# Where the sums of squares of the SwiGLU norm are made, when the first gate-and-up weights load, and which matmuls stand ahead of the last transposes

## The chip, the cores and the metric

The kernel runs on one core of a Trainium2 chip. The metric is device time in microseconds (us) of one execution; lower is better. Five engines work from queues of their own: TensorE (PE; its weight loads are PEld), VectorE (DVE), ScalarE (ACT), GpSimd (POOL) and SyncE (SP), which issues most transfers. Each runs its instructions in order and waits for the others by semaphores.

## The reference, cut to what matters

Two layers on 512 tokens of width 1024, in float32. Layer 0 mixes tokens with a dilated window attention, layer 1 with a gated linear attention (GLA); both end with a SwiGLU block of hidden width 2816:

```python
def rms_norm(x, gain):
    xf = x.astype(jnp.float32)
    y = xf * lax.rsqrt(jnp.mean(xf * xf, axis=-1, keepdims=True) + RMS_EPS)
    return (y * gain.astype(jnp.float32)).astype(x.dtype)

def swiglu(h, w_gate_up, w_down):
    g, u = jnp.split(h @ w_gate_up, 2, axis=-1)
    return (jax.nn.silu(g) * u) @ w_down

# in reference(), for each layer i
    h = h + mix.astype(h.dtype)
    h = h + swiglu(rms_norm(h, ffn_norm[i]), ffn_w_gate_up[i], ffn_w_down[i]).astype(h.dtype)
```

## The kernel before

**Products.** Each large product is float32 made of two halves: a hi half that ScalarE writes (a copy, L92) and a lo half that VectorE writes (source minus hi, L93). `split` makes both, and each block costs three matmuls: hi by hi, hi by lo, lo by hi (`mm3`, L104 to L106; `product`, L298 to L300).

**Layout.** The residual h lies transposed, as eight tiles of 128 features by 512 tokens. In `swiglu`, `gate_up` makes the hidden activations, `down` brings them back.

**The start of the block.** As each tile of h is finished (the attention's last adds at L767, the GLA's at L423), `enter_blocks` writes its gained operands (ScalarE L180, VectorE L181, tag xs), and `add_square` squares it on ScalarE (L151) and adds it on GpSimd to one tile, acc (L152). The norm's factor is applied to the products later, so the products don't wait for it by their data. `token_norm` sums acc over features with small matmuls (L205) into pt and makes R, the factor by token, in small steps on ScalarE and VectorE (L110 to L115, L208, L210). `block_sums` makes the sums of operands that the seven products need (ScalarE L192; VectorE L194 to L197, tag g; halves in sh and sl).

**Seven products.** `gate_up` runs six chunks of columns (five of 512, one of 256). In each, with tokens in halves and features in halves, seven products take the place of eight: A11 by first, A12 by second, then S1 by fifth, S2 by sixth, S4 by third, S3 by seventh, A22 by fourth, 24 matmuls each. `forms` makes the seven weights: SyncE loads blocks (wA, wf, wB), GpSimd's DMAs add a block into one that is there (L236), VectorE adds two (L267), and each is split. A load, add or split of `forms` gets a priority offset of AHEAD = 100 over what is written around it; a scheduler orders each engine's instructions from priorities and dependences. SiLU (L359, L381), the products with R (L371, L383) and the transposes of the activations (`turn`, L324, with a copy to an act at L330) follow; transposes of a chunk are made while the next chunk is multiplied. The token norm is called after the second product's matmuls of chunk 0; the scheduler puts its matmuls where acc allows. Three buffers each hold wh and wl, two wB.

**Down.** After chunk 5's last SiLU, `turn` transposes that chunk's two columns of blocks, and `down` splits all 22 activations (tag ah) and runs 66 matmuls for each of eight output tiles m, adding h, which is read back from DRAM (L408). In layer 0 each result enters the next mixer's norm, `enter_norm`, with `add_square` again.

## Time and profile before

| what | value |
|---|---|
| time of three runs | 1593.56, 1594.47, 1595.35 us; median 1594.47 |
| the profiled execution | 1593.73 us, its span 1592.0 us |
| mean granted TensorE clock | 0.991 |
| GpSimd's adds of squares (L152) | 21, 30.7 us together |
| ScalarE's squares (L151) | 21, 13.1 us together |
| transposes of activations (L324) | 176, 30.2 us together (16.4 + 13.8) |

Durations below are those of one profiled execution. A row of the timeline gives start, duration, engine, line, operation, what is written from what, and, in brackets, how long the engine was idle before it and what it waited for. A matmul's shown duration is its passage through the array; the distance between starts is what one costs. The granted clock is a share of full speed.

### The profile page before, as it was taken

To read this page: it belongs to the slowest core of one execution; us is meant where nothing else is said; L and a number is where in the kernel's file an instruction comes from. 1 tells how busy PE (TensorE), PEld (TensorE's weight loads), DVE (VectorE), ACT (ScalarE), POOL (GpSimd) and SP (SyncE) were. 2 spreads that over 40 slices of the span, in tenths; PEclk is the share of its full clock that TensorE was granted. 3 is DMA by queue.
4 is the path that set the end of the run, shared out by engine and by line. 5 is a ranking of instruction groups with operands and counts; after the bars stand their busy time and mean duration, and the time that the engine had idled before them with its cause. 6 is when DMAs were issued, how large, how long until landed. Compare 5 with 4: busy or idle time off the path is not lost.

```text
span 1592.0 us, 21064 instructions
## 1 busy us (share of the span) xinstructions
PE 1552.2 (97%) x8078; PEld 1258.5 (79%) x8078; DVE 947.0 (59%) x1693; ACT 779.0 (49%) x1319; POOL 134.3 (8%) x201
## 2 busy tenths in 40 slices
...
GB/s 277 139 73 88 69 79 87 60 121 97 80 67 48 70 44 178 126 159 159 159 160 113 125 100 85 95 67 66 67 69 215 136 154 158 155 149 123 113 120 65
DMA packets 58964, 179.74 MB, mean 113 GB/s; under 512 B 9936, under 2 KB 10512, under 8 KB 58864
## 3 DMA queue, kind: packets, MB, share of 16 engines
...
## 4 chain that ended last, share of the span: by engine, by line
PE 73%; issue 12%; DVE 7%; ACT 3%; DMA 2%; POOL 2%; SPq 0%; POOLq 0%; DVEq 0%; ACTq 0%
PE ppp L496 8%; PE ppp L494 8%; PE ppp L495 8%; PE ppp L105 7%; PE ppp L104 7%; PE ppp L106 7%; PE po L603 4%; PE ppp L298 3%; PE ppp L299 3%; PE ppp L300 3%; DMA wB<-in_gate_up_dram 2%; PE ps L671 2%; DVE wl L93 2%; PE pt L541 2%; PE ps L621 1%
## 5 line engine op out<-in xcount | busy, mean ns | idle before, releaser
L93 DVE TENSOR_TENSOR wl<-wf,wh 128x1024 fp32r<-128x1024 f32 (+1 forms) x180 | 214.7, 1193 | 212.2 <-ACT wh L92 211.2
L92 ACT ACTIVATE wh<-wf 128x1024 fp32r<-128x1024 f32 (+1 forms) x180 | 185.5, 1031 | 305.9 <-PE ppp L105 181.2
L494 PE MATMUL ppp<-wh,xs 128*128 128x512 f32 (+1 forms) x672 | 263.0, 393 | 5.6 <-ACT wh L92 5.6
L496 PE MATMUL ppp<-wh,xs 128*128 128x512 f32 (+1 forms) x672 | 262.8, 391 | 0.0
L495 PE MATMUL ppp<-wl,xs 128*128 128x512 f32 (+1 forms) x672 | 262.6, 391 | 0.0
L494 PEld LDWEIGHTS ppp<-wh,xs 128*128 128x128 f32 x672 | 128.0, 191 | 30.4 <-ACT wh L92 5.6
L496 PEld LDWEIGHTS ppp<-wh,xs 128*128 128x128 f32 x672 | 127.9, 190 | 23.4 <-issue 0.2
L495 PEld LDWEIGHTS ppp<-wl,xs 128*128 128x128 f32 x672 | 128.2, 191 | 22.2 <-DVE wl L93 1.2
L104 PE MATMUL ppp<-ah,wh 128*128 128x512 f32 x352 | 138.1, 393 | 2.2 <-ACT ah L92 2.2
L105 PE MATMUL ppp<-ah,wh 128*128 128x512 f32 x352 | 138.5, 394 | 0.5 <-DVE ah L93 0.5
L106 PE MATMUL ppp<-ah,wl 128*128 128x512 f32 x352 | 138.0, 392 | 0.0
L93 DVE TENSOR_TENSOR wl<-wA,wh 128x1024 fp32r<-128x1024 f32 x88 | 107.5, 1221 | 50.1 <-ACT wh L92 50.0
L92 ACT ACTIVATE wh<-wA 128x1024 fp32r<-128x1024 f32 x88 | 92.6, 1056 | 53.1 <-PE ppp L300 39.0
L299 PE MATMUL ppp<-wl,xs 128*128 128x512 f32 (+1 forms) x288 | 108.2, 376 | 1.2 <-DVE wl L93 1.2
L298 PE MATMUL ppp<-wh,xs 128*128 128x512 f32 (+1 forms) x288 | 108.5, 383 | 0.0
L300 PE MATMUL ppp<-wh,xs 128*128 128x512 f32 (+1 forms) x288 | 107.7, 375 | 0.0
L93 DVE TENSOR_TENSOR wl<-wB,wh 128x1024 fp32r<-128x1024 f32 x44 | 53.9, 1225 | 89.5 <-ACT wh L92 89.5
L105 PE MATMUL ppp<-xs,wh 128*128 128x512 f32 x224 | 91.1, 407 | 1.0 <-DVE xs L93 1.0
L104 PE MATMUL ppp<-xs,wh 128*128 128x512 f32 x224 | 91.1, 407 | 0.0
L106 PE MATMUL ppp<-xs,wl 128*128 128x512 f32 x224 | 90.2, 403 | 0.0
L104 PEld LDWEIGHTS ppp<-ah,wh 128*128 128x128 f32 x352 | 66.6, 189 | 16.5 <-ACT ah L92 2.7
L105 PEld LDWEIGHTS ppp<-ah,wh 128*128 128x128 f32 x352 | 66.9, 190 | 15.8 <-DVE ah L93 2.0
...
## 6 DMA issues: line engine op xcount, KB each, us to landing
...
```

Source lines behind the costliest of these rows:

```text
L92: nc.scalar.activation(hi, src, AF.Copy)
L93: nc.vector.tensor_sub(lo, src, hi.bitcast(F32))
L104: mm(out, lhsT=wh, rhs=xh, start=start, stop=False)
L105: mm(out, lhsT=wh, rhs=xl, start=False, stop=False)
L106: mm(out, lhsT=wl, rhs=xh, start=False, stop=stop)
L298: mm(a, lhsT=xh[:, tok], rhs=wh[:, f], start=start and k == 0, stop=False, skip_group_check=True)
L299: mm(a, lhsT=xh[:, tok], rhs=wl[:, f], start=False, stop=False, skip_group_check=True)
L300: mm(a, lhsT=xl[:, tok], rhs=wh[:, f], start=False, stop=k == last, skip_group_check=True)
L494: mm(a, lhsT=xh, rhs=wh[:, f], start=k == 0, stop=False)
L495: mm(a, lhsT=xh, rhs=wl[:, f], start=False, stop=False)
L496: mm(a, lhsT=xl, rhs=wh[:, f], start=False, stop=k == KT - 1)
L603: self.nc.tensor.matmul(o, lhsT=pts[b][c], rhs=vals(i0 + b, c), start=c == 0, stop=c == 1)
```

## The change

Three edits. (1) `enter_blocks` makes no squares; `gate_up` makes them in chunk 0 after the second product, in two buffers by turns (sq and R), and the add to acc is VectorE's, here and in layer 0's `down`. (2) Chunk 0's first weights get a priority offset of 300 instead of 100. (3) The first two activations are split in chunk 1's part of the program order, written at the end of chunk 4, into free xs buffers, and the six down matmuls on them for m = 0 are issued ahead of the last transposes; `down_part` holds the loop that `down` had.

```diff
--- before.py
+++ after.py
@@ -52,7 +52,7 @@
             "qv": 2, "qr": 2, "qtmp": 2, "st": 2, "t2": 2, "stn": 2, "st0": 2, "mw": 2, "mL": 5}
     FFN = {"a": NH - KT}
     GATE_UP = {"sh": 4, "sl": 4, "wA": 4, "wB": 2, "g": 7, "Rc": 8}
-    DOWN = {"ah": 2 * NH}
+    DOWN = {"ah": 2 * NH - 4}
     GLA = {"qk": 8, "r": 8, "v": 8, "wg": 1, "z": 1, "rs": 2, "A": 2, "qs": 6, "kT": 6, "e": 4, "y": 1, "c": 1, "wa": 3,
            "state": 6, "later": 1, "reset": 1, "Rc": 1, "mid": 2, "full": 4}
     PBUFS = {"pp": 4, "s": 2, "t": 1, "o": 1}
@@ -141,15 +141,15 @@
         self.x[m] = self.gained(src, col)
         self.add_square(m, src)
 
-    def add_square(self, m, src):
+    def add_square(self, m, src, tag="sq"):
         nc = self.nc
         if m == 0:
             self.acc = self.t("acc")
             nc.scalar.activation(self.acc, src, AF.Square)
         else:
-            sq = self.t("sq")
+            sq = self.t(tag)
             nc.scalar.activation(sq, src, AF.Square)
-            nc.gpsimd.tensor_add(self.acc, self.acc, sq)
+            nc.vector.tensor_add(self.acc, self.acc, sq)
 
     def column_sums(self, ps, src):
         hi, lo = self.split(src, (P, S), "e", "e")
@@ -180,7 +180,6 @@
         nc.scalar.activation(xh, part, AF.Copy, scale=col)
         nc.vector.scalar_tensor_tensor(xl, part, col, xh.bitcast(F32), op0=ALU.mult, op1=ALU.subtract)
         self.x[m] = (xh, xl)
-        self.add_square(m, src)
 
     def block_sums(self, m):
         nc = self.nc
@@ -219,7 +218,7 @@
             with self.phase(f"down{layer}", self.DOWN):
                 self.down(layer, acts, col_next)
 
-    def forms(self, dram):
+    def forms(self, dram, ahead=0):
         nc = self.nc
         n = dram.shape[1]
         raw = {}
@@ -280,8 +279,9 @@
             return ready("wA")
 
         for step in (first, second, fifth, sixth, third, seventh, fourth):
-            with self.tc.high_priority(offset=AHEAD):
+            with self.tc.high_priority(offset=AHEAD + ahead):
                 w = step()
+            ahead = 0
             yield w
 
     def product(self, acc, x, w, width, start):
@@ -303,7 +303,7 @@
         nc = self.nc
         self.col0 = 16 + 8 * layer
         ACT, DVE = nc.scalar.activation, nc.vector
-        weights = [self.forms(self.ins["gate_up"][layer, j]) for j in range(5)]
+        weights = [self.forms(self.ins["gate_up"][layer, j], 0 if j else 2 * AHEAD) for j in range(5)]
         weights.append(self.forms(self.ins["gate_up_last"][layer]))
         first = next(weights[0])
         self.minus = self.t("Rc", (P, 8))
@@ -350,6 +350,8 @@
             self.product(b2, A12, next(w), width, True)
             turn(1)
             if j == 0:
+                for m in range(KT):
+                    self.add_square(m, self.h[m], ("sq", "R")[m % 2])
                 R = self.token_norm()
                 for m in range(KT):
                     nc.gpsimd.dma_start(self.kept[m], self.h[m])
@@ -382,28 +384,41 @@
                 u = h2[:, i, 0:width]
                 DVE.scalar_tensor_tensor(u, u, R[:, 6 + i:7 + i], e, op0=ALU.mult, op1=ALU.mult)
             done = (h1, h2)
+            if j == 4:
+                with self.tc.high_priority(offset=AHEAD):
+                    early = [self.split(a, (P, S), "xs", "xs") for a in acts[0:2]]
+        self.started = self.down_part(self.p("pp"), layer, 0, 0, 2, early)
         for c in range(2):
             turn(c)
         with self.tc.issue_after(silu.ins):
             nc.scalar.preload_act_table_set("natural_log_exp_and_others")
 
+    def down_part(self, ps, layer, m, k, end, pairs):
+        for k0, kn in ((0, 8), (8, 8), (16, 6)):
+            if k0 <= k < min(end, k0 + kn):
+                if k == k0:
+                    self.down_w = self.weight(self.ins["down"][layer, m, :, k0 * P:(k0 + kn) * P], kn * P)
+                wh, wl = self.down_w
+                while k < min(end, k0 + kn):
+                    c = slice((k - k0) * P, (k - k0 + 1) * P)
+                    self.mm3(ps, wh[:, c], wl[:, c], *pairs[k], k == 0, k == NH - 1)
+                    k += 1
+        return ps, pairs
+
     def down(self, layer, acts, col_next):
         nc = self.nc
-        pairs = []
-        for k, a in enumerate(acts):
+        ps, pairs = self.started
+        for k in range(2, NH):
             if k < 8:
                 with self.tc.high_priority(offset=AHEAD):
-                    pairs.append(self.split(a, (P, S), "ah", "ah"))
+                    pairs.append(self.split(acts[k], (P, S), "ah", "ah"))
             else:
-                pairs.append(self.split(a, (P, S), "ah", "ah"))
+                pairs.append(self.split(acts[k], (P, S), "ah", "ah"))
         self.x = [None] * KT
         for m in range(KT):
-            ps = self.p("pp")
-            for k0, kn in ((0, 8), (8, 8), (16, 6)):
-                wh, wl = self.weight(self.ins["down"][layer, m, :, k0 * P:(k0 + kn) * P], kn * P)
-                for k in range(k0, k0 + kn):
-                    c = slice((k - k0) * P, (k - k0 + 1) * P)
-                    self.mm3(ps, wh[:, c], wl[:, c], *pairs[k], k == 0, k == NH - 1)
+            if m > 0:
+                ps = self.p("pp")
+            self.down_part(ps, layer, m, 2 if m == 0 else 0, NH, pairs)
             h = self.t("h")
             nc.sync.dma_start(h, self.kept[m])
             self.h[m] = h
```

Lines after some 150 shift by one to three, and `down` by more. The following rows are each engine's order in the program, without times: line, operation, what is written from what.

TensorE at the start of `gate_up` in layer 0, before: the attention's last matmul, the token norm (pt from ones and acc), the first product.

```order
L106 MATMUL ppp_1123_5917<-qk_1051_5577,wl_1110_5869 128x512
L205 MATMUL pt_1161_6065<-ones_4_73,acc_1098_5822 128x1 x4
L298 MATMUL ppp_1150_5998<-wh_1129_5943,xs_1097_5819 128x512
L298 MATMUL ppp_1151_5999<-wh_1129_5943,xs_1097_5819 128x512
L299 MATMUL ppp_1150_5998<-wl_1130_5944,xs_1097_5819 128x512
L300 MATMUL ppp_1150_5998<-wh_1129_5943,xs_1097_5819 128x512
```

After the change the first product follows the attention directly:

```order
L106 MATMUL ppp_1116_5897<-qk_1051_5577,wl_1106_5858 128x512
L298 MATMUL ppp_1142_5975<-wh_1121_5920,xs_1097_5819 128x512
L298 MATMUL ppp_1143_5976<-wh_1121_5920,xs_1097_5819 128x512
L299 MATMUL ppp_1142_5975<-wl_1122_5921,xs_1097_5819 128x512
L300 MATMUL ppp_1142_5975<-wh_1121_5920,xs_1097_5819 128x512
```

and the token norm stands inside product S4 (acc pair ps, operands sh):

```order
L300 MATMUL ps_1165_6093<-wh_1179_6175,sl_1133_5949 128x512
L298 MATMUL ps_1166_6094<-wh_1179_6175,sh_1132_5948 128x512
L204 MATMUL pt_1161_6065<-ones_4_73,acc_1153_6042 128x1 x4
L299 MATMUL ps_1166_6094<-wl_1180_6176,sh_1132_5948 128x512
L300 MATMUL ps_1166_6094<-wh_1179_6175,sl_1133_5949 128x512
L298 MATMUL ps_1165_6093<-wh_1181_6179,sh_1136_5959 128x512
```

The token norm moved back by 106 rows, from ahead of the first product into the fifth that is issued.

VectorE in the same chunk, at products S1 to S4, before (wl and sl are lo halves of weights and operand sums, Rc the norm's small tiles):

```order
L93 TENSOR_TENSOR wl_1175_6139<-wA_1127_5939,wh_1174_6138 128x1024
L93 TENSOR_TENSOR sl_1149_5994<-g_1147_5988,sh_1148_5993 128x1024
L93 TENSOR_TENSOR wl_1177_6143<-wA_1128_5941,wh_1176_6142 128x1024
L208 TENSOR_SCALAR Rc_1162_6070<-pt_1161_6065 128x4
L358 TENSOR_TENSOR g_1152_6024<-ppp_1153_6027,g_1152_6024 128x512
L358 TENSOR_TENSOR g_1152_6024<-ppp_1154_6028,g_1152_6024 128x512
L93 TENSOR_TENSOR wl_1180_6176<-wB_1167_6097,wh_1179_6175 128x1024
L93 TENSOR_TENSOR wl_1182_6180<-wB_1168_6099,wh_1181_6179 128x1024
```

and after:

```order
L93 TENSOR_TENSOR sl_1141_5971<-g_1139_5965,sh_1140_5970 128x1024
L93 TENSOR_TENSOR wl_1175_6139<-wA_1119_5916,wh_1174_6138 128x1024
L93 TENSOR_TENSOR wl_1177_6143<-wA_1120_5918,wh_1176_6142 128x1024
L152 TENSOR_TENSOR acc_1153_6042<-acc_1153_6042,R_1156_6050 128x512
L93 TENSOR_TENSOR wl_1180_6176<-wB_1167_6097,wh_1179_6175 128x1024
L152 TENSOR_TENSOR acc_1153_6042<-acc_1153_6042,sq_1157_6053 128x512
L360 TENSOR_TENSOR g_1144_6001<-ppp_1145_6004,g_1144_6001 128x512
L152 TENSOR_TENSOR acc_1153_6042<-acc_1153_6042,R_1158_6056 128x512
L93 TENSOR_TENSOR wl_1182_6180<-wB_1168_6099,wh_1181_6179 128x1024
L152 TENSOR_TENSOR acc_1153_6042<-acc_1153_6042,sq_1159_6059 128x512
L360 TENSOR_TENSOR g_1144_6001<-ppp_1146_6005,g_1144_6001 128x512
L152 TENSOR_TENSOR acc_1153_6042<-acc_1153_6042,R_1160_6062 128x512
```

Five adds to acc stand between the low halves of the weights, and sl of the fourth operand sum stands one low half sooner.

ScalarE in chunk 0 of layer 1, before (wh from wB is the hi half of S4's weights first; ACT_TABLE_LOAD changes the table of functions):

```order
L110 ACT_TABLE_LOAD
L110 ACTIVATE Rc_2034_10575<-Rc_2033_10574 128x4
L92 ACTIVATE wh_2047_10646<-wA_1999_10445 128x1024
L111 ACT_TABLE_LOAD
L111 ACTIVATE Rc_2034_10575<-Rc_2034_10575 128x4
L342 ACTIVATE g_2044_10637<-ps_2036_10597 128x512
L92 ACTIVATE wh_2050_10679<-wB_2038_10601 128x1024
L342 ACTIVATE g_2044_10637<-ps_2037_10598 128x512
L359 ACT_TABLE_LOAD
L359 ACTIVATE g_2023_10528<-g_2023_10528,Rc_2034_10575 128x512
L92 ACTIVATE wh_2052_10683<-wB_2039_10603 128x1024
```

and after:

```order
L92 ACTIVATE wh_2045_10642<-wA_1990_10420 128x1024
L92 ACTIVATE wh_2047_10646<-wA_1991_10422 128x1024
L342 ACTIVATE g_2044_10637<-ps_2036_10597 128x512
L92 ACTIVATE wh_2050_10679<-wB_2038_10601 128x1024
L342 ACTIVATE g_2044_10637<-ps_2037_10598 128x512
L92 ACTIVATE wh_2052_10683<-wB_2039_10603 128x1024
L110 ACT_TABLE_LOAD
L110 ACTIVATE Rc_2034_10575<-Rc_2033_10574 128x4
L342 ACTIVATE g_2049_10674<-ppp_2013_10479 128x512
L111 ACT_TABLE_LOAD
```

Both hi halves of wB stand ahead of the table loads now.

TensorE at the end of `gate_up` and the start of `down` in layer 0, before:

```order
L300 MATMUL ppp_1406_7508<-wh_1440_7745,xs_1125_5926 128x256
L324 MATMUL pt_1443_7778<-ident_2_65,g_1434_7676 128x128
L324 MATMUL po_1445_7785<-ident_2_65,g_1434_7676 128x128 x2
L324 MATMUL pt_1443_7778<-ident_2_65,g_1439_7740 128x128
L324 MATMUL po_1445_7785<-ident_2_65,g_1439_7740 128x128
L324 MATMUL pt_1443_7778<-ident_2_65,g_1439_7740 128x128
L324 MATMUL po_1445_7785<-ident_2_65,g_1439_7740 128x128
L104 MATMUL ppp_1491_7885<-ah_1447_7797,wh_1493_7888 128x512
L105 MATMUL ppp_1491_7885<-ah_1448_7798,wh_1493_7888 128x512
```

and after (xs here holds the halves of an activation):

```order
L300 MATMUL ppp_1410_7516<-wh_1444_7753,xs_1118_5906 128x256
L105 MATMUL ppp_1447_7786<-xs_1406_7508,wh_1449_7789 128x512
L106 MATMUL ppp_1447_7786<-xs_1405_7507,wl_1450_7790 128x512
L104 MATMUL ppp_1447_7786<-xs_1407_7511,wh_1449_7789 128x512
L105 MATMUL ppp_1447_7786<-xs_1408_7512,wh_1449_7789 128x512
L106 MATMUL ppp_1447_7786<-xs_1407_7511,wl_1450_7790 128x512
L324 MATMUL pt_1451_7799<-ident_2_65,g_1438_7684 128x128 x2
L324 MATMUL pt_1451_7799<-ident_2_65,g_1443_7748 128x128
L324 MATMUL po_1453_7806<-ident_2_65,g_1438_7684 128x128 x2
L324 MATMUL po_1453_7806<-ident_2_65,g_1443_7748 128x128
L324 MATMUL pt_1451_7799<-ident_2_65,g_1443_7748 128x128
L324 MATMUL po_1453_7806<-ident_2_65,g_1443_7748 128x128
```

Five down matmuls moved ahead of the transposes, and the sixth, the first L104, stands ahead of product A22, outside these rows. SyncE's reads of h for m = 0 and 1 (`down`, h from h_dram) moved ahead of chunk 3's loads of wB, in both layers.

## The prediction

> **What bounds the kernel now.** I read the page first, for the engine that sets the end.
>
> ```profile
> span 1592.0 us, 21064 instructions
> PE 1552.2 (97%) x8078; PEld 1258.5 (79%) x8078; DVE 947.0 (59%) x1693; ACT 779.0 (49%) x1319; POOL 134.3 (8%) x201
> PE 73%; issue 12%; DVE 7%; ACT 3%; DMA 2%; POOL 2%; SPq 0%; POOLq 0%; DVEq 0%; ACTq 0%
> ```
>
> The second line is busy time by engine, the third the chain that ended last. TensorE is busy for 97% of the span, so only some 40 us of it are idle, and the change removes no matmul. It can win only what TensorE idles, or works at a low clock, at the places that it touches. There are three, each twice, once a layer: the start of gate-and-up, its product S3 (weights "seventh"), and the start of down. I went through TensorE's timeline there, then through the engines that it waits for. Columns: start, duration, engine, line, and in brackets the idle time before and what ended it.
>
> ```profile
> 629.84 0.39 PE L106 MATMUL ppp<-qk,wl 128*128 128x512 f32 x1
> 638.27 1.87 PE L205 MATMUL pt<-ones,acc 128*128 128x1 f32 x8 [8.04 <-POOL acc L152]
> 641.55 0.80 PE L299 MATMUL ppp<-wl,xs 128*128 128x512 f32 x1 [0.35 <-DVE wl L93]
> 645.22 0.39 PE L300 MATMUL ppp<-wh,xs 128*128 128x512 f32 x1
> 645.45 0.40 PE L298 MATMUL ppp<-wh,xs 128*128 128x512 f32 x1
> ```
>
> That is the start in layer 0. TensorE ends the attention's last product at 629.84 and sits 8.04 us until GpSimd's last sum of squares lets the token norm (L205) go. The norm is not the whole hold: the first product still waits for VectorE's low half of the first weight (L93) at 641.55. So the time to beat is 641.55, not 638.27. At full clock a matmul starts every 0.23 us (645.22 to 645.45).
>
> ```profile
> 630.26 0.68 DVE L767 TENSOR_TENSOR h<-ppp,h 128x512 f32<-128x512 f32 x1
> 631.10 1.25 DVE L181 SCALAR_TENSOR_TENSOR xs<-h,cols,xs 128x512 fp32r<-128x512 f32 x1 [0.16 <-ACT xs L180]
> ...
> 636.35 0.74 DVE L181 SCALAR_TENSOR_TENSOR xs<-h,cols,xs 128x512 fp32r<-128x512 f32 x1
> 637.02 1.49 DVE L196 SCALAR_TENSOR_TENSOR g<-g,g 128x256 f32<-128x256 f32 x1
> ...
> 639.55 0.41 DVE L196 SCALAR_TENSOR_TENSOR g<-g,g 128x256 f32<-128x256 f32 x1
> ...
> 640.28 1.21 DVE L93 TENSOR_TENSOR wl<-wA,wh 128x1024 fp32r<-128x1024 f32 x1
> 636.56 1.66 POOL L152 TENSOR_TENSOR acc<-acc,sq 128x512 f32<-128x512 f32 x1 [0.23 <-ACT sq L151]
> 637.61 1.04 ACT L92 ACTIVATE wh<-wA 128x1024 fp32r<-128x1024 f32 x1
> ```
>
> VectorE is slow here while GpSimd adds. The same operand (L181) takes 1.25 us at 631.10 and 0.74 at 636.35; the same sum (L196) 1.49 at 637.02, beside GpSimd's add at 636.56, and 0.41 at 639.55. In the view of waits, cut to 628 to 645 us, ScalarE waits for GpSimd too (total, times, mean):
>
> ```profile
> ACT sq L151 <- POOL acc L152: 3.1, 5, 0.8
> ```
>
> **Start of gate-and-up, layer 0.** The squares leave the stretch, and with them GpSimd's adds. VectorE's order after its last h add (630.26) is: two operands L181, one tiny step and eight short ones on g, then the first weight's low half. I rebuild it from the short durations. The h add cannot end before TensorE's last product, about 631.0. Two operands at about 0.67 a step, one tiny step 0.1 and eight g steps at 0.34 to 0.4 before the low half make some 4.4 us, and L93 adds 1.2: 636.6 instead of 641.49, **-4.9**. ScalarE's hi half, 637.61 now, needs the last h too, then two operands and three copies; without the waits above it is ready near 634, so VectorE stays last. TensorE still idles for five us, so I let it restart at half clock as now and run perhaps two more slow matmuls: +0.5. Of the seven adds two fall among the h adds, where VectorE waits for TensorE, and five behind the second product. Net -4.4.
>
> The larger offset on the first weights costs and wins nothing by itself: in layer 0 the first weight's halves keep their place behind the operands.
>
> **Token norm.** It now stands inside product S4 in layer 0 and S2 in layer 1. Before, its eight small matmuls lay under a wait in layer 0; now they interrupt full-rate work.
>
> ```profile
> 1242.07 0.95 PE L205 MATMUL pt<-ones,acc 128*128 128x1 f32 x8
> L533 DVE TENSOR_TENSOR wa<-wa,wb 128x512 f32<-128x512 f32 x48 | 32.8, 684 | 0.1
> L152 POOL TENSOR_TENSOR acc<-acc,sq 128x512 f32<-128x512 f32 x21 | 30.7, 1461 | 137.8 <-ACT sq L151 84.7 <-issue 53.1
> ```
>
> The layer 1 row is the warm price, 0.95 us for eight: +0.9 in layer 0, nothing in layer 1, where it was paid already. The trace shows no VectorE add of acc; the nearest row, L533, is the same shape at 684 ns against 1461 on GpSimd. Five adds between the low halves in chunk 0 are 3.4 us of VectorE, in a stage where the next fence shows it waiting for weights. Bounds: nothing, if all lie in waits; 3.4 us a layer, if none does. I take 0.3 a layer, near the first end, since the adds stand before S4's and S3's low halves, and S3's wait for a DMA anyway. The seven adds that enter layer 0's down are free: nothing there reads acc until the next mixer's norm.
>
> **Product S3.**
>
> ```profile
> 663.61 0.85 POOL L236 DMA_DIRECT2D wB<-in_gate_up_dram  x1 [1.55 <-DVE wl L93]
> 669.94 1.06 ACT L92 ACTIVATE wh<-wB 128x1024 fp32r<-128x1024 f32 x1 [2.33 <-DMA wB<-in_gate_up_dram]
> 671.05 0.50 PE L298 MATMUL ppp<-wh,sh 128*128 128x512 f32 x1 [0.67 <-ACT wh L92]
> 672.31 0.50 PE L299 MATMUL ppp<-wl,sh 128*128 128x512 f32 x1 [0.76 <-DVE wl L93]
> 675.85 0.50 PE L299 MATMUL ppp<-wl,sh 128*128 128x512 f32 x1 [0.49 <-DVE wl L93]
> 1250.32 1.28 ACT L111 ACT_TABLE_LOAD   x1
> 1252.20 1.05 ACT L92 ACTIVATE wh<-wB 128x1024 fp32r<-128x1024 f32 x1
> 1261.41 1.06 ACT L92 ACTIVATE wh<-wB 128x1024 fp32r<-128x1024 f32 x1 [4.08 <-DMA wB<-in_gate_up_dram]
> 1263.01 0.50 PE L298 MATMUL ppp<-wh,sh 128*128 128x512 f32 x1 [2.17 <-ACT g L342]
> ```
>
> S3's weights are wB plus a block that a GpSimd DMA adds into it; that DMA starts when wB's old content has been split, and everything from there is a chain: issue 663.61, hi half 669.94, matmul 671.05. In layer 0 TensorE loses 0.67 + 0.76 + 0.49 = 1.9 us, with the restarts some 2.4. After the change S4 is 0.9 longer, and the low half of S1's last operand stands one step (1.2) sooner on VectorE, so the chain gains up to two us on TensorE; the adds put the second wB half back. I take -1.8. In layer 1 two table loads (1250.32 is the second, 1.28 each) stand ahead of wB's hi half at 1252.20; after, both hi halves stand ahead of all loads, so the chain starts up to 2.5 sooner and the 2.17 can go. The DMAs share one queue, so I take -2.2.
>
> **Start of gate-and-up, layer 1.**
>
> ```profile
> 1235.88 0.50 PE L299 MATMUL ppp<-wl,xs 128*128 128x512 f32 x1 [0.31 <-DVE wl L93]
> 1239.45 0.50 PE L299 MATMUL ppp<-wl,xs 128*128 128x512 f32 x1 [0.56 <-DVE wl L93]
> ```
>
> Only 0.31 + 0.56, with restarts about 1.2, and with GpSimd's last add of acc gone from beside them I take -1.0. Together: layer 0 -4.4 + 0.9 + 0.3 - 1.8 = **-5.0**, layer 1 -2.2 - 1.0 + 0.3 = **-2.9**.
>
> **Start of down.**
>
> ```profile
> 870.61 0.33 PE L324 MATMUL pt<-ident,g 128*128 128x128 f32 x1 [1.16 <-DVE g L383]
> 872.14 0.50 PE L104 MATMUL ppp<-ah,wh 128*128 128x512 f32 x1 [1.09 <-ACT ah L92]
> 873.45 0.60 PE L104 MATMUL ppp<-ah,wh 128*128 128x512 f32 x1
> ...
> 876.97 0.40 PE L106 MATMUL ppp<-ah,wl 128*128 128x512 f32 x1
> 1465.94 0.49 PE L104 MATMUL ppp<-ah,wh 128*128 128x512 f32 x1 [1.10 <-ACT ah L92]
> ```
>
> The last transposes wait 1.16 us for VectorE's L383, the first down matmul 1.09 for its operand, and layer 1 reads the same. Six matmuls move into that wait: 6 x 0.23 = 1.36, less 0.23 for the one that stands ahead of product A22 and so delays the chain to L383: **-1.1 each**, -2.2. The six have their operands split in chunk 1; the two splits there cost ScalarE and VectorE no work in sum. SyncE's reloads of h for m = 0 and 1 move ahead of chunk 3's wB loads, two without a wait: nothing.
>
> The rest is the clock. From 873.45 to 876.97 eight matmuls take 3.5 us where 1.8 would do: 1.7 lost. The view of windows (busy by engine, then the granted clock, DMA share, GB/s) shows why:
>
> ```profile
> 874.00:876.00 2.00, 2.00 (x6) 1.61 (x6) 2.00 (x4) 2.00 (x5) 0.00 (x0) 0.50 0.83 245
> 1264.00:1268.00 4.00, 3.75 (x16) 2.78 (x16) 3.17 (x4) 3.00 (x3) 0.00 (x0) 1.00 0.36 136
> ```
>
> The clock falls to half after 868 to 873 us, where TensorE idles 2.9 of five, but stayed full after the single gap of 2.17 at 1263.01. With six matmuls put in, about 1.6 of the five remain idle: between the two cases, nearer the second. I forecast one of the two starts at full clock: -1.7. Bounds: nothing and -3.4. By the Trainium skill (TensorE: Matmul & The Clock Gate, Part 1: The HAM clock gate), the clock halves after an idle window of a free-running 3.4 us and returns after a busy one, so whether a short gap trips it depends on where it falls; the trace agrees in the half clock of 3.5 us after 873.45. By that rule alone a start that keeps any cold window gives the rival "both cold" below.
>
> **Sum:** -5.0 - 2.9 - 2.2 - 1.7 = **-11.8 us** against the profiled execution's 1593.73 (span 1592.0 and 1.7 around it), 1581.9. The median of the runs shown is 1594.47, 0.74 above, so I forecast **1582.7**.
>
> **Rivals.** The price of a square, from the groups by line, is used in the last of them.
>
> ```profile
> L151 ACT ACTIVATE sq<-h 128x512 f32<-128x512 f32 x21 | 13.1, 624 | 5.2 <-POOL acc L152 4.2 <-DVE h L423 1.0
> ```
>
> *Both down starts stay cold:* no -1.7, **1584.4**. For it: the two starts read alike now, gap for gap, so they may fall alike later; by the same token both may turn warm, 1581.0. *VectorE becomes the bound in chunk 0:* the adds cost their upper bound, 3.4 instead of 0.3 a layer, **1588.9**; its low halves (L93) end five of the waits quoted above; against it, it is busy for only 59% of the span. *The start is held elsewhere:* ScalarE's hi half or a weight buffer holds it, and only the down parts and layer 0's S3 remain, less the norm: 1594.47 - 2.2 - 1.8 + 0.9 = **1591.4**. *Slower:* the late squares use two buffers in turn, so ScalarE's square (L151, 0.62) waits for VectorE's add of two before, and the add for the square; between them on both queues stand weight halves (1.05 and 1.21 above). One add stands ahead of the low half of the first wB and two more ahead of that of the second. If each costs a full round of square, add and one half on either engine, 0.62 + 0.68 + 1.05 + 1.21 = 3.6, the second wB's DMA starts 10.7 us later, and S3 stands still behind it for that and 1.7 at half clock: 12.4 a layer less the 2 that S4's norm and today's wait absorb, 1582.7 + 2 x 10.4 = **1603.5**. It decides from (11.8 + 3.2) / 2 = 7.5 us a layer. For it: S3's chain hangs on that DMA now. Against it: the squares need only h, and ScalarE has 2.33 us of idle before 669.94 alone; at the bare price of add and square the delay is near 2.7.
>
> **How the numbers follow.** Forecast 0.50 (with both warm), both cold 0.20, VectorE the bound 0.15, start held elsewhere 0.09, slower 0.06. 0.2% is 3.2 us, about what a measurement of this kernel can tell from no change: the first three lie beyond it, the fourth at -3.1 is just within, the last beyond it on the other side. Faster 0.85, same 0.09, slower 0.06. The range: down to both warm with the gate-and-up waits all gone (2 us more), 1578.5; up to VectorE as the bound, 1589.5.
>
> **What would show it.** In the new profile: TensorE's first L299 of layer 0's chunk 0 about five us sooner after the attention's last matmul; no GpSimd add; VectorE's L181 at 0.74 throughout; the token norm without idle before it, 0.95 for eight; S3's first matmul waiting under 0.7 in both layers; six matmuls ahead of the last transposes, and clock 1.00 or 0.50 in the two us behind them. A wait of the token norm for VectorE's acc, or of S4 or S3 for a low half behind an add, would make the forecast wrong.

## The result, and the profile after

| kernel | median (lowest to highest), us | runs |
|---|---|---|
| before | 1594.01 (1592.17 to 1595.35) | 4 |
| changed | 1585.28 (1582.96 to 1586.52) | 4 |

The ratio is 0.9944, with a 95% interval of 0.9927 to 0.9962: the change makes the kernel 8.7 us faster. The forecast was 1582.7, 11.8 below the kernel before, in a range of 1578.5 to 1589.5. The time fell into the range and the sign is as forecast, but 3 of the 12 us are missing, and the parts of the sum came out quite unlike what they were given.

The changed kernel was profiled three times in all, once here and twice more beside the experiments. In the first profile the span is 1581.2 us, 1592.0 before. Busy time by engine on its page:

```profile
PE 1550.1 (98%) x8078; PEld 1257.4 (80%) x8078; DVE 949.4 (60%) x1714; ACT 780.0 (49%) x1319; POOL 104.1 (7%) x180
```

GpSimd has lost its 21 adds and 30 us, and VectorE has 21 instructions more and is only 2.4 us busier. TensorE's timeline of layer 0's start, from the attention's last product on:

```profile
627.99 0.39 PE L106 MATMUL ppp<-qk,wl 128*128 128x512 f32 x1
...
634.61 0.79 PE L299 MATMUL ppp<-wl,xs 128*128 128x512 f32 x1 [1.30 <-DVE wl L93]
```

The view by source line has the operand L181 on VectorE (lowest, median and highest ns of one):

```profile
L181 DVE SCALAR_TENSOR_TENSOR xs<-h,cols,xs x16: 475/612/746, 620.2 to 1226.6; 128x256 fp32r<-128x256 f32 x8, 128x512 fp32r<-128x512 f32 x8
```

The first L299 now starts 634.61 - 627.99 = 6.62 us after the attention's last matmul, 11.71 before. No L181 takes over 0.746 us; its longest was 1.776. What ends the wait is what ended it before, VectorE's low half of the first weight, only 5.1 us sooner. The next fence has the token norm and the products S3 and A22 of layer 0, and behind them, from the timelines of GpSimd and ScalarE, the first and the last of the four adding DMAs, the two hi halves of wB, which wait for the last two of them, and what ScalarE does behind the second half (L361 is the first SiLU, L342 the copy of S3's sums).

```profile
659.66 1.01 PE L204 MATMUL pt<-ones,acc 128*128 128x1 f32 x8
665.36 0.50 PE L299 MATMUL ppp<-wl,sh 128*128 128x512 f32 x1 [0.76 <-DVE wl L93]
668.36 0.49 PE L298 MATMUL ppp<-wh,sh 128*128 128x512 f32 x1 [0.23 <-ACT wh L92]
669.62 0.50 PE L299 MATMUL ppp<-wl,sh 128*128 128x512 f32 x1 [0.76 <-DVE wl L93]
673.38 0.50 PE L298 MATMUL ppp<-wh,xs 128*128 128x512 f32 x1 [0.86 <-ACT g L342]
652.19 0.85 POOL L235 DMA_DIRECT2D wA<-in_gate_up_dram  x1 [14.19 <-DVE wl L93]
...
658.00 0.85 POOL L235 DMA_DIRECT2D wB<-in_gate_up_dram  x1 [2.09 <-DVE wl L93]
662.99 1.06 ACT L92 ACTIVATE wh<-wB 128x1024 fp32r<-128x1024 f32 x1 [4.78 <-DMA wB<-in_gate_up_dram]
667.25 1.06 ACT L92 ACTIVATE wh<-wB 128x1024 fp32r<-128x1024 f32 x1 [1.39 <-DMA wB<-in_gate_up_dram]
668.32 1.28 ACT L361 ACT_TABLE_LOAD   x1
669.62 1.34 ACT L361 ACTIVATE g<-g,Rc 128x512 f32<-128x512 f32 x2
672.75 0.57 ACT L342 ACTIVATE g<-ppp 128x512 f32<-128x512 f32 x1
```

The norm costs 1.01 and waits for nothing. But S3 and A22 now wait 0.76 + 0.23 + 0.76 + 0.86 = 2.6 us, where before it was 0.67 + 0.76 + 0.49 = 1.9. The first three are S3's and go back to wB: ScalarE waits 4.78 us for the first half and 1.39 for the second, and VectorE's low halves wait for ScalarE's (4.57 and 1.49 us), not behind an add. The last, A22's, is of another kind. It waits for ScalarE's copy of S3's sums, which stands behind a table load and the two first SiLUs, 2.6 us together. SiLU needs R, and R comes later now; before, the same table load stood at 665.59, ahead of the first half at 669.94, and A22 waited for nothing. In layer 1 the same stretch has gained. ScalarE's timeline there:

```profile
1244.24 1.06 ACT L92 ACTIVATE wh<-wB 128x1024 fp32r<-128x1024 f32 x1 [2.34 <-PE ppp L300]
1245.32 1.28 ACT L110 ACT_TABLE_LOAD   x1
1250.47 1.06 ACT L92 ACTIVATE wh<-wB 128x1024 fp32r<-128x1024 f32 x1 [1.16 <-DMA wB<-in_gate_up_dram]
```

Both hi halves of the old wB now stand ahead of the table loads, and the wait for the new one, 4.08 us before, is 1.16. Last, the start of down in layer 0 on TensorE's timeline:

```profile
866.61 0.33 PE L324 MATMUL pt<-ident,g 128*128 128x128 f32 x1 [0.52 <-DVE g L385]
868.14 0.50 PE L104 MATMUL ppp<-ah,wh 128*128 128x512 f32 x1 [1.10 <-ACT ah L92]
```

The view of windows behind the starts of both layers (stretch, its length, busy time of PE, PEld, DVE, ACT and POOL with counts, granted clock, DMA share, GB/s):

```profile
870.00:872.00 2.00, 2.00 (x5) 1.61 (x6) 2.00 (x4) 2.00 (x5) 0.00 (x0) 0.50 0.82 199
1460.00:1462.00 2.00, 2.00 (x11) 1.67 (x10) 2.00 (x4) 1.65 (x4) 0.00 (x0) 1.00 0.66 206
```

The six early matmuls cut the first wait from 1.16 to 0.52 and leave the second at 1.10; layer 1 reads the same. Layer 0's down goes on at half clock, layer 1's at full clock.

To see where the 8.7 us went I cut each trace at the same TensorE instructions. Chunk 0 counts from the attention's (GLA's) last matmul to chunk 1's first; a start of down from chunk 5's last product matmul to the 73rd TensorE instruction behind it. The difference is the changed kernel's first profile less before's, the mean that of its three profiles.

| stage, us | before | changed, three profiles | difference | of the mean |
|---|---|---|---|---|
| up to the attention's last matmul (not touched) | 629.8 | 628.0, 632.1, 628.3 | -1.9 | -0.4 |
| layer 0, chunk 0 | 54.4 | 51.0, 49.8, 50.2 | -3.4 | -4.1 |
| layer 0, chunks 1 to 4 | 161.5 | 162.7, 165.1, 164.2 | +1.2 | +2.5 |
| layer 0, start of down | 21.2 | 20.4, 20.4, 20.2 | -0.8 | -0.9 |
| layer 0's down from there on, and GLA | 340.3 | 339.2, 339.1, 339.1 | -1.1 | -1.1 |
| layer 1, chunk 0 | 46.0 | 42.0, 41.4, 41.2 | -3.9 | -4.4 |
| layer 1, chunks 1 to 4 | 164.1 | 165.5, 167.0, 166.0 | +1.4 | +2.1 |
| layer 1, start of down | 21.3 | 18.9, 20.5, 19.0 | -2.4 | -1.8 |

The rows left out (chunk 5 of both layers, 22.2 to 22.3 us, and the rest of layer 1's down) differ by some 0.1 us each. The differences add up to -10.9, and the span fell by 10.8. The stages that the change touches give back some 12 us, and chunks 1 to 4 take 2.6 (first profile) to 4.5 (mean) of them away again. The first row says how far one profile can be trusted: 630 us that are the same program in all kernels came out between 628.0 and 632.1.

### The profile page after: what moved, and what is told of

It reads as the page before. It is cut to its first block, busy times and chain, and to the rows that moved or that the text cites. A ratio compares the mean times of both kernels' runs of the same rounds, so it can differ in the third digit from the quotient of the medians.

```text
span 1581.2 us, 21054 instructions
## 1 busy us (share of the span) xinstructions
PE 1550.1 (98%) x8078; PEld 1257.4 (80%) x8078; DVE 949.4 (60%) x1714; ACT 780.0 (49%) x1319; POOL 104.1 (7%) x180
## 4 chain that ended last, share of the span: by engine, by line
PE 75%; issue 13%; DVE 5%; ACT 3%; DMA 2%; POOL 2%; POOLq 0%; SPq 0%; ACTq 0%; DVEq 0%
PE ppp L511 8%; PE ppp L509 8%; PE ppp L510 8%; PE ppp L105 8%; PE ppp L104 8%; PE ppp L106 8%; PE po L618 4%; PE ppp L298 3%; PE ppp L299 3%; PE ppp L300 3%; DMA wB<-in_gate_up_dram 2%; PE ps L686 2%; PE pt L556 1%; PE ps L636 1%; PE po L938 1%
## 5 line engine op out<-in xcount | busy, mean ns | idle before, releaser
L511 PEld LDWEIGHTS ppp<-wh,xs 128*128 128x128 f32 x672 | 128.1, 191 | 23.4
L104 PE MATMUL ppp<-ah,wh 128*128 128x512 f32 x320 | 125.6, 392 | 2.2 <-ACT ah L92 2.2
L105 PE MATMUL ppp<-ah,wh 128*128 128x512 f32 x320 | 125.7, 393 | 0.5 <-DVE ah L93 0.5
L106 PE MATMUL ppp<-ah,wl 128*128 128x512 f32 x320 | 125.0, 391 | 0.0
L299 PE MATMUL ppp<-wl,xs 128*128 128x512 f32 (+1 forms) x288 | 107.9, 375 | 1.3 <-DVE wl L93 1.3
L105 PE MATMUL ppp<-xs,wh 128*128 128x512 f32 x256 | 103.7, 405 | 1.1 <-DVE xs L93 1.1
L104 PE MATMUL ppp<-xs,wh 128*128 128x512 f32 x256 | 103.4, 405 | 0.0
L106 PE MATMUL ppp<-xs,wl 128*128 128x512 f32 x256 | 102.9, 402 | 0.0
L583 ACT ACTIVATE sm<-sm,st 128x160 f32<-128x160 f32 (+2 forms) x128 | 56.9, 446 | 43.0 <-DVE st L582 41.5
L299 PE MATMUL ppp<-wl,sh 128*128 128x512 f32 (+1 forms) x192 | 73.0, 380 | 4.7 <-DVE wl L93 4.7
```

The costliest lines, as they stand in the source:

```text
L104: mm(out, lhsT=wh, rhs=xh, start=start, stop=False)
L105: mm(out, lhsT=wh, rhs=xl, start=False, stop=False)
L106: mm(out, lhsT=wl, rhs=xh, start=False, stop=stop)
L299: mm(a, lhsT=xh[:, tok], rhs=wl[:, f], start=False, stop=False, skip_group_check=True)
L511: mm(a, lhsT=xl, rhs=wh[:, f], start=False, stop=k == KT - 1)
```

## The experiments

"Before" below is the kernel before as it ran on the same chip beside the kernels of one table; its medians were 1596.55 (first table), 1597.72 (second), 1598.85 (third) and 1596.87 (beside `fill_down`). Each ratio is to the one beside it.

### Which edit gives the gain

Four kernels ran side by side. `swap_only` is the kernel before with VectorE's adds:

```diff
-            nc.gpsimd.tensor_add(self.acc, self.acc, sq)
+            nc.vector.tensor_add(self.acc, self.acc, sq)
```

> The kernel before with one edit: the adds to acc go to VectorE; the squares stay where they were, and nothing of down is moved. Theory A (the gain at gate-and-up comes from taking the adds off GpSimd, where they slow VectorE and end late): layer 0's first L299 stands 6 to 7.5 us after the attention's last matmul (before 11.7, changed kernel 6.6), S3 with its neighbours gains rather than loses, since no add stands ahead of wB's low halves, the next mixer's norm after down starts about 1.1 sooner; time 7 to 10 us below before. Theory B (the late place of the squares is what frees the start): seven adds now stand in VectorE's own chain there and the norm still holds the first product, so the first L299 stands at 9 us or later, and the time is at most 4 us below before.

`defer_pool` is the changed kernel with that line turned back: the squares are late, the adds on GpSimd.

```diff
-            nc.vector.tensor_add(self.acc, self.acc, sq)
+            nc.gpsimd.tensor_add(self.acc, self.acc, sq)
```

> The changed kernel with one edit undone: the adds to acc are back on GpSimd, the squares stay late. Theory A: GpSimd's adds still run beside the start; first L299 10 us or more after the attention's last matmul, and the gain at gate-and-up (7.4 us in the two layers) is mostly gone; time 2 to 5 us below before, which is the down part. Theory B: the start keeps its gain, first L299 by 8 us; time within 3 us of the changed kernel.

`down_only` is the third edit alone, written as the changed kernel with the others undone:

```diff
-            nc.vector.tensor_add(self.acc, self.acc, sq)
+            nc.gpsimd.tensor_add(self.acc, self.acc, sq)
...
         self.x[m] = (xh, xl)
+        self.add_square(m, src)
...
-        weights = [self.forms(self.ins["gate_up"][layer, j], 0 if j else 2 * AHEAD) for j in range(5)]
+        weights = [self.forms(self.ins["gate_up"][layer, j], 0) for j in range(5)]
...
-                for m in range(KT):
-                    self.add_square(m, self.h[m], ("sq", "R")[m % 2])
```

> The kernel before with the third edit alone: two early splits and six down matmuls ahead of the last transposes. Both theories: each down start 1.1 us shorter at the same clock, and 1.7 more where it no longer falls to half clock; gate-and-up unchanged; time 2.2 to 5.6 us below before.

`swap_down` is `down_only` with VectorE's adds, so the change without the late squares and the offset.

> The first and the third of these together: adds on VectorE, squares at their old place, six down matmuls early. Theory A: the sum of both, 10 to 13 us below before and 1 to 4 below the changed kernel, as S3 of chunk 0 no longer waits behind the adds. Theory B: 4 to 8 below before, slower than the changed kernel.

| kernel | median (range), us | ratio to before, 95% interval |
|---|---|---|
| swap_only | 1588.35 (1587.10 to 1589.03) | 0.9956 [0.9939, 0.9973] |
| defer_pool | 1595.23 (1590.93 to 1603.38) | 1.0001 [0.9985, 1.0018] |
| down_only | 1596.90 (1590.35 to 1599.34) | 0.9993 [0.9975, 1.0011] |
| swap_down | 1586.20 (1584.54 to 1589.58) | 0.9946 [0.9926, 0.9967] |

One word, `vector` for `gpsimd`, is worth 8.2 us by the medians; the late squares without it are worth nothing. TensorE's timeline after the attention's last matmul, first in `swap_only`, then in `defer_pool`, and one VectorE row of the latter:

```profile
631.05 0.39 PE L106 MATMUL ppp<-qk,wl 128*128 128x512 f32 x1
637.00 0.79 PE L299 MATMUL ppp<-wl,xs 128*128 128x512 f32 x1 [0.63 <-DVE wl L93]
```

```profile
632.20 0.39 PE L106 MATMUL ppp<-qk,wl 128*128 128x512 f32 x1
639.22 1.87 PE L204 MATMUL pt<-ones,acc 128*128 128x1 f32 x8 [6.63 <-POOL acc L152]
643.49 0.80 PE L299 MATMUL ppp<-wl,xs 128*128 128x512 f32 x1 [1.34 <-DVE wl L93]
634.59 1.26 DVE L181 SCALAR_TENSOR_TENSOR xs<-h,cols,xs 128x512 fp32r<-128x512 f32 x1
```

With the squares at their old place but VectorE's adds, the first L299 starts 5.95 us behind; with late squares and GpSimd's adds, 11.29, and L181 takes 1.26 again. That they are written behind the second product did not move them: they still run beside the start, TensorE still waits for acc there, and the slow VectorE steps come back with GpSimd's adds. So the start's gain is the engine, not the place. (In `swap_only` the norm itself waits for nothing either: with the faster adds it stands behind the second product, at 650.40.)

Layer 1 reads the same way. ScalarE's timeline in `defer_pool`, then in `swap_only`, around the old wB's first hi half and the new one's:

```profile
1252.18 1.28 ACT L111 ACT_TABLE_LOAD   x1
1254.06 1.05 ACT L92 ACTIVATE wh<-wB 128x1024 fp32r<-128x1024 f32 x1
1263.39 1.06 ACT L92 ACTIVATE wh<-wB 128x1024 fp32r<-128x1024 f32 x1 [4.20 <-DMA wB<-in_gate_up_dram]
```

```profile
1248.19 1.05 ACT L92 ACTIVATE wh<-wB 128x1024 fp32r<-128x1024 f32 x1
1249.26 1.28 ACT L110 ACT_TABLE_LOAD   x1
1257.39 1.06 ACT L92 ACTIVATE wh<-wB 128x1024 fp32r<-128x1024 f32 x1 [0.67 <-DMA wB<-in_gate_up_dram]
```

`defer_pool` keeps the tables ahead of wB and the wait of 4.20; its chunk 0 takes 46.2 us, as before. `swap_only` has moved the first hi half ahead of them, and takes 43.0. The late squares on VectorE, on top, bring layer 1 from 42.2 in `swap_down` to 41.2 to 42.0 and layer 0 from 52.0 to 49.8 to 51.0: some 1 us a layer, seen in the stages only and with one profile of `swap_down`. The totals of `swap_only` and `swap_down` do not tell the third edit apart. `down_only` has its gain in the stages, 20.2 us a start where before has 21.2 and 21.3, but its total, expected 2.2 to 5.6 us lower, is lost in before's spread of 12 us here (1589.94 to 1601.69). The changed kernel did not run beside these four. Its own ratios were 0.9944 above and 0.9907 and 0.9902 in the tables below, so how much the other edits add to `swap_only`'s 0.9956 in total time is not settled: between next to nothing (beside 0.9944) and half of the gain (beside 0.9902).

The second edit does nothing: with an offset of 100 in place of 300 the built program is the same, so it was not run.

### Why S3 did not gain

Three theories: the second wB DMA is issued late, behind the adds; the four adding DMAs share a queue that needs its time, whatever stands around them; or TensorE's restart at half clock, ahead of the first product. `wb_first` issues the wB pair ahead of the wA pair.

```diff
-                nc.gpsimd.dma_start(raw[tag][i], dram[block, i], accum_op=ALU.add)
+                raw["last"] = nc.gpsimd.dma_start(raw[tag][i], dram[block, i], accum_op=ALU.add)
...
         def third():
-            add("wA", 1)
             return ready("wC")
...
                 add("wB", 2)
+                with self.tc.issue_after(raw["last"].ins):
+                    add("wA", 1)
+            else:
+                add("wA", 1)
```

> The changed kernel with one edit: in every chunk GpSimd issues the two adding DMAs into wB (S3's weights) ahead of the two into wA (A22's), instead of behind them. Theory C (chunk 0 gives back part of its sooner start at S3, since wB's DMAs come last of four on one queue, whose landings the start does not move): wB lands 4 to 5 us sooner against S1's end, S3 runs in 5.4 to 6.5 us instead of 9.3 in layer 0 and 7.8 in layer 1, chunk 0 takes 46.5 to 49 us (51.0) and 39.5 to 41 (42.0), and chunk 4's wait at S3 goes too: 5 to 9 us below the changed kernel. Theory D (the adds to acc ahead of wB's low halves delay S3): the second half of S3 still waits, and the gain is under 2 us.

`behind_wb` makes squares, adds and norm stand behind the old wB's low halves, and with them the first SiLU of chunk 0:

```diff
+            third = next(w)
+            low = self.low
+            self.product(b3, S4, third, width, False)
+            if j == 0:
+                for m in range(KT):
+                    with self.tc.issue_after(low.ins):
+                        self.add_square(m, self.h[m], ("sq", "R")[m % 2])
+                R = self.token_norm()
...
+                    silu = ACT(e, e, AF.Silu, scale=R[:, i:i + 1])
```

> The changed kernel with the squares, their adds and the token norm behind the low halves of wB in chunk 0 (seven adds in one place, norm in S3 or later), the order of the DMAs unchanged. Theory C: the second DMA into wB is issued 1.5 us sooner against the first but lands within 1 us of where it did, and S3 gains at most 1 us; the norm's late R costs nothing or up to 1 us. Theory D: S3 loses its second wait, 1.5 to 2.5 us a layer, time 3 to 5 below the changed kernel.

`swap_wb` is `swap_down` with the edit of `wb_first`, so the old place of the squares.

> Adds on VectorE, squares at their old place, six down matmuls early, and the wB DMAs first. Theory C: chunk 0 gains at S3 as in the run with the changed kernel; since this one starts as early but waits 1.7 us in S1 for operand sums, it ends within 2 us of that run, 4 to 8 below the changed kernel. Theory D: no gain from the order, within 2 us of the same kernel without it (1586.2).

`after_again` is the changed kernel, unedited, beside them.

> The changed kernel once more, beside the others: 1583 to 1587; the two down starts 18.9 us each where the clock stays full and 20.4 where it falls, likely one or both at half clock; S3 of layer 0's chunk 0 at 9 us again, within 0.5; chunk 4's S3 waits come and go by a microsecond.

| kernel | median (range), us | ratio to before, 95% interval |
|---|---|---|
| wb_first | 1611.65 (1606.12 to 1614.87) | 1.0091 [1.0066, 1.0117] |
| behind_wb | 1590.72 (1586.09 to 1594.29) | 0.9951 [0.9932, 0.9970] |
| swap_wb | 1607.66 (1603.84 to 1618.02) | 1.0065 [1.0041, 1.0090] |
| after_again | 1581.25 (1580.08 to 1590.56) | 0.9907 [0.9875, 0.9939] |

All three are slower than the changed kernel beside them, two of them slower than the kernel before. ScalarE's and then TensorE's timeline of `wb_first`:

```profile
663.50 1.06 ACT L92 ACTIVATE wh<-wB 128x1024 fp32r<-128x1024 f32 x1 [2.05 <-DMA wB<-in_gate_up_dram]
666.62 1.06 ACT L92 ACTIVATE wh<-wB 128x1024 fp32r<-128x1024 f32 x1 [0.26 <-DMA wB<-in_gate_up_dram]
672.62 1.06 ACT L92 ACTIVATE wh<-wA 128x1024 fp32r<-128x1024 f32 x1 [1.33 <-DMA wA<-in_gate_up_dram]
674.21 0.50 PE L301 MATMUL ppp<-wh,xs 128*128 128x512 f32 x1 [1.46 <-ACT g L345]
717.19 0.50 PE L301 MATMUL ppp<-wh,xs 128*128 128x512 f32 x1 [2.61 <-ACT g L345]
```

The wB halves come together, and in layer 0's chunk 0 S3 runs without a wait for them; that chunk takes 48.9 us, 0.9 less than the changed kernel's best. But the wA pair comes last now. ScalarE waits 1.33 us for one of its blocks, the copy that A22 needs stands behind that, and A22 waits 1.46 us in chunk 0 and, by the same order, 2.61 in chunk 1. Layer 1's chunk 0 takes 44.9, 2.9 more than the changed kernel's longest. Layer 0's chunks 1 to 4 take 172.7 us instead of 162.7 to 165.1, layer 1's 173.5. Whichever pair goes last, its product waits: the queue is what is short. `swap_wb` says the same without the late squares.

TensorE's timeline in `behind_wb` at the norm of both layers:

```profile
677.93 1.02 PE L204 MATMUL pt<-ones,acc 128*128 128x1 f32 x8 [0.81 <-DVE acc L152]
1266.04 1.26 PE L204 MATMUL pt<-ones,acc 128*128 128x1 f32 x8 [2.48 <-DVE acc L152]
```

In layer 0 S3 shrinks to 6.5 us: the first of the four DMAs is issued 23.4 us behind the attention's last matmul, 24.2 to 24.7 in the changed kernel. But the norm is now what TensorE waits for, 0.81 and 2.48, and layer 1's chunk 0 takes 47.2. Put behind wB, acc is ready too late.

### What the adds and the cold starts cost

`no_late_adds` squares three tiles instead of eight and so makes two adds instead of seven: the norm lacks five eighths of its sum, and its matmuls stand right behind the attention's again.

```diff
-                for m in range(KT):
+                for m in range(3):
                     self.add_square(m, self.h[m], ("sq", "R")[m % 2])
```

> The changed kernel with only the first three tiles of h squared into acc (so the norm lacks five eighths of the sum, and stands ahead of the first product): no add and no late square stands near wB's halves, and no norm in S4. Theory C (the queue of four adding DMAs bounds S3 in chunk 0): TensorE comes to S3 0.9 us sooner and waits that much more; S3 with its waits takes 7.5 us or more in layer 0 and chunk 0 ends within 1 us of the changed kernel's 49.8 to 51.0. Theory D (the adds and squares hold wB's low halves): S3 takes under 6.5 us, chunk 0 47.5 or less.

`keep_warm` gives TensorE matmuls that nobody reads, in two of its waits: 14 ahead of layer 0's first product, 4 between the last transposes and down.

```diff
+    def fill(self, count, lhsT, rhs):
+        ps = self.p("s")
+        with self.tc.issue_after(self.last_mm.ins):
+            for i in range(count):
+                self.last_mm = self.nc.tensor.matmul(ps, lhsT=lhsT, rhs=rhs, start=True, stop=True)
...
+            if j == 0 and layer == 0:
+                self.fill(14, self.x[0][0][:, 0:P], self.x[4][0])
...
+        self.fill(4, early[0][0][:, 0:P], early[1][0])
```

> The changed kernel with matmuls that nothing reads put into TensorE's waits: 14 between the attention's last matmul and the first product of layer 0, 4 between the last transposes and the first down matmul, in both layers. If TensorE's idle time there is what drops the clock: no half clock at the layer 0 start (now 6.8 us of it) nor at the two down starts, which take 18.9 to 19.2 us each (20.4); 3 to 5 us below the changed kernel. If idle time is not the cause, or the 8 to 12 small gaps that remain suffice: the same half clock, and the time is the changed kernel's, or up to 1 us above.

`after_third` is the changed kernel, unedited, beside these two.

> The changed kernel beside it: 1580 to 1587, down starts 20.4 where the clock falls, 18.9 where not.

`fill_down`, which ran later and beside the kernel before alone, is `keep_warm` without the 14:

```diff
+        self.fill(4, early[0][0][:, 0:P], early[1][0])
```

> The changed kernel with the four unread matmuls ahead of the first down matmul in both layers, and without the fourteen at the layer 0 start. If the fill keeps the clock (it did at both starts in the run with both fills), the two down starts take 18.9 us each where the changed kernel has 18.9 to 20.5, and nothing else moves: 0 to 3 us below the changed kernel, ratio to before 0.988 to 0.991. If the clock falls all the same, the time is the changed kernel's.

| kernel | median (range), us | ratio to before, 95% interval |
|---|---|---|
| no_late_adds | 1583.83 (1582.71 to 1588.66) | 0.9909 [0.9890, 0.9928] |
| keep_warm | 1584.49 (1582.55 to 1589.54) | 0.9909 [0.9892, 0.9927] |
| after_third | 1583.21 (1580.91 to 1586.65) | 0.9902 [0.9887, 0.9917] |
| fill_down | 1582.16 (1579.39 to 1583.23) | 0.9912 [0.9890, 0.9933] |

**The adds cost nothing that can be measured.** With five of the seven gone, and the norm out of S4, the time is the same. S3 still waits, and for the same DMAs. GpSimd's first issue in chunk 0, ScalarE's second new wB half and S3's longest wait in `no_late_adds`:

```profile
655.80 0.85 POOL L235 DMA_DIRECT2D wA<-in_gate_up_dram  x1 [14.43 <-DVE wl L93]
669.41 1.06 ACT L92 ACTIVATE wh<-wB 128x1024 fp32r<-128x1024 f32 x1 [0.50 <-DMA wB<-in_gate_up_dram]
668.48 0.63 PE L298 MATMUL ppp<-wh,sh 128*128 128x512 f32 x1 [1.88 <-ACT g L342]
```

The 1.88 us are for a copy of ScalarE's that stands behind the first new wB half, and that half waited 4.69 us for its DMA. A22 waits for nothing here: the norm is early, and so is SiLU. The last of the four DMAs, at 658.00 in the changed kernel's first profile, is issued 30.0 us after the attention's last matmul there, and 29.7 here by the same view (661.09 - 631.35): without the adds it is no sooner. From the first issue to the half that the last of the four lets go it is 669.41 - 655.80 = 13.6 us. In the changed kernel it is 667.25 - 652.19 = 15.1, and 13.4 and 14.0 in its other profiles; the kernel before has 14.5. Its first and last issue, then ScalarE's table load, ahead of both new wB halves, and the second half:

```profile
658.94 0.85 POOL L236 DMA_DIRECT2D wA<-in_gate_up_dram  x1 [14.00 <-DVE wl L93]
665.01 0.85 POOL L236 DMA_DIRECT2D wB<-in_gate_up_dram  x1 [0.54 <-DVE Rc L113]
665.59 1.28 ACT L359 ACT_TABLE_LOAD   x1
673.48 1.06 ACT L92 ACTIVATE wh<-wB 128x1024 fp32r<-128x1024 f32 x1 [1.87 <-DMA wB<-in_gate_up_dram]
```

So before, the last DMA was issued 665.01 - 629.84 = 35.2 us after the attention's last matmul, 30.0 after the change: 5.2 sooner. What counts is the half behind it: 43.6 us before, 39.3, 38.1 and 38.4 in the changed kernel's three profiles, so 4.4, 5.6 and 5.2 sooner. S4's last matmul, and with it TensorE's arrival at S3, moved from 40.2 to 35.6, 36.2 and 35.8, so 4.6, 4.0 and 4.3 sooner. The chain has moved with TensorE and gained 0.8 us on it in the mean, in the first profile nothing; the transfers themselves are no quicker.

**Matmuls in the first wait win nothing.** TensorE's timeline of `keep_warm`, from the 14 to the first matmul of a lo half (L305 there, L299 above), and after it the view of windows from there on, columns as above:

```profile
631.15 3.33 PE L291 MATMUL ps<-xs,xs 128*128 128x512 f32 x14
635.03 0.73 PE L304 MATMUL ppp<-wh,xs 128*128 128x512 f32 x2 [0.54 <-ACT wh L92]
637.55 0.80 PE L305 MATMUL ppp<-wl,xs 128*128 128x512 f32 x1 [1.79 <-DVE wl L93]
```

```profile
637.00:640.00 3.00, 2.45 (x6) 1.97 (x7) 3.00 (x4) 1.89 (x3) 0.90 (x1) 0.53 0.29 22
```

The attention's last matmul is at 630.93 there, so the L305 starts 6.62 us behind it, as in the changed kernel to the hundredth: VectorE's low half of the first weight holds it. The two short waits that are left, 0.54 and 1.79, are enough for the clock to fall (0.53 behind them). Chunk 0 took 53.4 us, 2.4 to 3.7 more than in the changed kernel's profiles, with TensorE stopped 1.87 us ahead of A22 for VectorE's products with R, and at half clock behind that; `fill_down`, without the 14, has 49.9. Why the fill should cost anything 40 us later is not explained by one profile, and this was the slowest of the six executions (1589.54 us). Four of the others had a mean granted clock of 0.995 to 0.997, more than any execution of the changed kernel (0.989 to 0.994), so less half clock; where it went is not recorded. They took 1582.55 to 1584.64 us, within the changed kernel's 1580.91 to 1586.65 beside them. So the third theory, that the half clock of the restart holds S3 back, was not put to a clean test, but nothing speaks for it.

**The clock at down's start is a matter of idle time.** Four unread matmuls take 0.9 us there. TensorE's timeline in `fill_down` at layer 0's down:

```profile
868.03 1.18 PE L291 MATMUL ps<-xs,xs 128*128 128x512 f32 x4
869.37 0.51 PE L104 MATMUL ppp<-ah,wh 128*128 128x512 f32 x1 [0.16 <-ACT ah L92]
```

The view of windows of `fill_down` behind both starts, columns as above:

```profile
871.00:873.00 2.00, 1.95 (x9) 1.58 (x9) 2.00 (x5) 2.00 (x5) 0.00 (x0) 1.00 0.73 164
1456.00:1458.00 2.00, 2.00 (x10) 1.63 (x10) 2.00 (x4) 2.00 (x5) 0.00 (x0) 1.00 0.72 193
```

The wait of 1.10 is 0.16, and the clock stays at 1.00 at both starts, in `keep_warm` too: four of four. Without the fill the changed kernel had full clock at two of six (layer 1 of its first and third profile), and all kernels here that have the third edit and no fill, the changed kernel among them, at five of twenty. The starts take 18.9 to 19.0 us with it, up to the same matmul of down and the four counted in, against 18.9 to 19.0 (full clock) and 20.2 to 20.5 (half clock) without. The Trainium skill (TensorE: Matmul & The Clock Gate, Part 1: The HAM clock gate) says that the gate looks at windows of 3.4 us that run freely; the stretches of half clock in these traces last 3.4, 6.8 or 10.2 us, which agrees. No single wait at these starts is longer than 1.2 us; in sum TensorE idles 2.9 us there before, 1.8 with the six matmuls and 0.9 with the fill. `fill_down` has the shortest profile of all, 1577.6 us of span, but its ratio does not set it apart from the changed kernel, whose own ratios were 0.9907 and 0.9902 in the tables above.

## Why the prediction was right, and where it was wrong

**Start in layer 0: right, its size too small.** The forecast was -4.9 for the first L299 and, with 0.5 for a slow restart, -4.4 net. It gave -5.1 at the first L299, and -5.3, -4.7 and -5.3 at the second product's first matmul (13.1, 13.7 and 13.1 us after the attention's last, 18.4 before), so the 0.5 is seen in one profile of three. `swap_only` and `defer_pool` show that the engine of the adds makes this gain. That it works through VectorE, as forecast, is read from L181: 1.25 us beside GpSimd's adds, under 0.75 without them. ScalarE's waits for GpSimd, 3.1 us, went with them and were not separated. The prediction put it down to the squares leaving the stretch; written later but still on GpSimd, they gave 0.4 us (11.29 instead of 11.71).

**Token norm: right.** 1.01 us where 0.9 was forecast, no wait before it.

**The adds on VectorE: right to be cheap, still too dear.** 0.3 a layer was forecast, 3.4 was the rival; taking five of chunk 0's seven away changed nothing that can be measured. The rival "slower" expected them to put off the second wB's DMA by 10.7 us; it was issued 5.2 sooner, and no low half of S3 stood behind an add.

**S3 in layer 0: this step failed.** "After the change S4 is 0.9 longer, and the low half of S1's last operand stands one step (1.2) sooner on VectorE, so the chain gains up to two us on TensorE" was priced at -1.8. The chain gained 0.8 on TensorE in the mean, and S3's waits for wB went from 1.9 to 1.9, 0.8 and 1.3 us. The issues wait for the old blocks to be split, and those splits stand in the queues behind what TensorE has let go: the first issue came 4.4 to 4.9 us sooner, S2's first matmul 4.7 to 5.3. What is then left is the queue's own time, which neither the place of the squares, nor their number, nor the order of the pairs made shorter as a whole. And the prediction left out what the late norm does to ScalarE: with R late, the table load and the first SiLUs fall between wB's second half and A22's weights, and A22 waits 0.83 to 0.86 us in all three profiles. It waits 0.88 in `fill_down`, and 0.12 or less in every kernel with an early norm and the old order of the DMAs (before, `swap_only`, `swap_down`, `down_only`, `defer_pool`, `no_late_adds`). From S4's first matmul to A22's it took 16.0, 14.2 and 15.0 us, 13.9 before: +1.2 in the mean, of which the norm is 1.0, where +0.9 + 0.3 - 1.8 = -0.6 was forecast. Layer 0's chunk 0 came to -4.1 in the mean, -5.0 forecast; it is no further off because the start gave more than its term.

**Layer 1's chunk 0: right, too small.** -2.9 was forecast, -3.9 to -4.8 measured. Up to S4's first matmul it is -1.8 where -1.0 was forecast; S4 and S3 together give -2.1 to -3.0 where -2.2 was. The hi halves did move ahead of the table loads; but the first of them does so by the swap alone, with which the chunk takes 43.0 instead of 46.0, and the late squares add some 1.

**Down: the six matmuls right, the clock over-sized.** -1.1 a start was forecast; at half clock a start fell from 21.2 to 21.3 to 20.2 to 20.5, so 0.9. A full clock is worth 1.4 to 1.5 a start, not 1.7. "I forecast one of the two starts at full clock: -1.7" held in the first profile, where layer 1's start is -2.4; over three profiles it is two of six starts, so some -1.0 for both together. Of the rivals, "both starts cold" held in the second profile.

**The next mixer's norm: a term that I left out.** "The seven adds that enter layer 0's down are free" is wrong in the good direction. In the kernel before, the last of them is on the path, in timeline rows of GpSimd, ScalarE and TensorE:

```profile
997.38 1.42 POOL L152 TENSOR_TENSOR acc<-acc,sq 128x512 f32<-128x512 f32 x1 [14.53 <-ACT sq L151]
998.83 0.63 ACT L92 ACTIVATE e<-acc 128x512 fp32r<-128x512 f32 x1 [1.52 <-POOL acc L152]
999.51 0.50 PE L156 MATMUL ps<-e,ones 128*128 128x512 f32 x1 [0.48 <-ACT e L92]
```

An add of 1.42 us ends the layer, ScalarE waits 1.52 for it and TensorE for ScalarE. Every kernel with VectorE's adds has 339.0 to 339.2 us for this stage; the kernel before, `down_only` and `defer_pool` 340.3 to 341.1. That is -1.1.

**Chunks 1 to 4: not in the sum, and not settled.** They took 1.2 to 3.6 us more in layer 0 and 1.4 to 2.9 more in layer 1 than in the one profile of before. The waits stand in S3 of chunk 4, for the last wB, and vary from profile to profile; stretches of half clock fall there too. `fill_down`, with the same order of work in these chunks, has 162.1 and 163.2, the first 0.6 above before's, the second 0.9 below it. So it may be chance; one profile of before cannot say. With the mean stages -12.4 for what the change touches and these +4.5 the sum is -7.9, beside the medians' -8.7 above. That the -12.4 lies so near the forecast -11.8 is luck: layer 0's chunk 0 and the starts of down gave 0.9 and 1.2 us less than forecast, layer 1's chunk 0 and the next norm 1.5 and 1.1 more. The later tables have more, 0.9907 and 0.9902, so 16.5 and 15.6 us by the medians there, beside a slower kernel before. Why it gains more there stays open.
